# Splitting the output projection's weights half a chunk per attention round

## The chip, the cores and the metric

The kernel runs on one core of a Trainium2 chip. The core has five engines that run side by side and meet through semaphores: TensorE (PE, matrix multiplies and transposes), VectorE (DVE), ScalarE (ACT), GpSimd (POOL) and SyncE (SP, which issues most of the DMAs). The metric is the device time of one execution in microseconds; lower is better.

## The reference

One encoder layer with two kinds of attention side by side, applied to 1024 prompt tokens and 256 sample tokens with the same weights. All arithmetic is float32. What matters here, cut to its core:

```python
n = rms_norm(h, g_mix);  z = n @ w_in               # queries, keys, values of both kinds
oa = diff_attention(qa, ka, va, lam, slopes)        # 4 heads, two softmax maps each, ALiBi distance
oa = rms_norm(oa, g_subln) * (1 - lam_init)
ob = gqa_attention(qb, kb, vb)                      # 8 query heads on 2 key/value heads, rotary positions
h = h + concat([oa, ob]) @ w_out                    # the output projection: this case's stage
h = h + relu(rms_norm(h) @ w_ff1)**2 @ w_ff2        # MLP, 4096 wide
h = h + sigmoid(rms_norm(h) @ w_gate) * (p @ w_proj)
return rms_norm(h, g_final)
```

The output projection multiplies 1280 x 1024 activations by the 1024 x 1024 matrix `w_out`. Its 1024 rows are eight chunks of 128 rows, one for each pair of heads (`ch` 0 to 3 for the differential heads, 4 to 7 for the grouped ones).

## The kernel before, in words

**Precision by splitting.** TensorE multiplies a rounded float32 format (`F32R`) at full rate. To keep float32 accuracy every operand is split into `hi` (the rounded value) and `lo` (what is left), and each product becomes three matmuls: hi x hi, hi x lo, lo x hi. A split of a weight takes a copy on ScalarE and a subtraction on GpSimd.

**Stages.** The input projections come first. Then the attention runs with two kinds of side work woven into it: the rest of the input projection (`qk_rest`) and the output projection (`out_proj`). After the attention the rest of the output projection is woven with the norm and the transposes for the MLP; then the MLP, the gate and the final norm.

**Rounds.** The attention is written out by hand as a list of rounds (L1037 to L1057). A unit is 256 queries of one head; a unit over the 1024 prompt tokens covers four rounds with its transposes (`tr`, L696) and its value matmuls (`av`, L720). Its scores (`sc`, L642) and softmax (L655 or L659, L664 or L667, L675 to L681) run four to seven rounds earlier. The loop runs rounds 3 to 217.

**Filler.** In each round, between the score part and the value part, the loop takes side work from one generator. It may take as much as the round's own matmuls are worth times a ratio: 0.43, and 0.6 from round 160 on (`RATIO`, `RATIO2`, `LATE`). Side work comes in steps of three matmuls of 512 columns, worth 648 ns to the loop (L257). A generator that yields 0.0 ends the side work of that round, and what the round still had to give is forfeited (L1051 to L1053). So each `yield 0.0` means: the rest is for the next round.

**The output projection in two passes.** The first pass (chunks 0, 1, 4, 5) runs when the first half of the heads is done, the second (2, 3, 6, 7) when all are. In a pass, each of ten 128-token tiles takes two halves of 512 output columns; a half is 12 matmuls (four chunks, three products each), then an addition into `h` on VectorE (L942), and a `yield 0.0`. The matmuls are recorded under line 255 (`mm_gen`) with the tile name `pso`. Their PSUM banks come from the pool `pj` (two banks), which the `av` tiles use too.

**A chunk's weights.** `opw_dma` (L862) loads a chunk in two halves of 512 columns; `opw_split` (L874) takes one of five pairs of buffers and splits the two halves: per half a copy on ScalarE (L883) and a subtraction on GpSimd (L884). All of it is written into one round. In the first pass, the constant `Y` puts one `yield 0.0` ahead of the second, third and fourth split, and one ahead of the first tile. Two splits of the second pass are done ahead, inside the first pass, after its tiles 2 and 5 (`ahead`, L948); the last two are done at the start of the second pass, after two `yield 0.0` (L915 to L919). The first two splits of the first pass fall into rounds 104 and 105.

**The order on each engine.** What the code writes first has priority, but the framework orders each engine's instructions itself, with a timeline that it works out when the kernel is built (`schedule_with_timeline_sim`, L1680). So the order seen in the trace can differ from the written one. Loads go through SyncE's queue in order.

**After the rounds.** The loop at L1213 drains what is left of `out_proj`. With each finished tile (`op_done`) a norm (`mlp_norm`, ScalarE and VectorE), and then transposes into the MLP's operands become possible.

Of the kernel before, what the change touches and what calls it, by code (L numbers as in the profile page):

```python
# [40 lines left out]
def f(ap):  # L41
    return ap.bitcast(F32)
# [3 lines left out]
def encoder_kernel(ctx: ExitStack, tc: tile.TileContext, x, xT, pT, w_in, w_out, w_ff1, w_ff2, w_gate, w_proj,  # L46
# [5 lines left out]
    Y = (0, 1, 1)  # L52
# [143 lines left out]
    def slot(tag, shape, dt, name):  # L196
        return slot_pool[tag].tile(shape, dt, tag=tag, name=name, bufs=1)
# [54 lines left out]
    def mm_gen(ps, pairs, step=6):  # L252
        n = len(pairs)
        for i, (a, b) in enumerate(pairs):
            PE.matmul(ps, a, b, start=i == 0, stop=i == n - 1)  # L255
            if i % step == step - 1:
                yield step * ps.free_size() * 0.422  # L257
        if n % step:
            yield (n % step) * ps.free_size() * 0.422
# [280 lines left out]
    def flush():  # L540
        todo, deferred[:] = deferred[:], []
        for fn in todo:
            fn()
# [270 lines left out]
    def qk_rest():  # L814
        w = qk_split(qk_dma(0))
        for n, (h, col, dst, sc) in enumerate(qk_items):
            more = n + 1 < len(qk_items)
            raws = qk_dma(n + 1) if more else None
            wh, wl = w
            for ci, (c0, cn) in enumerate(TCH):  # L820
                ps = pj("psa")
                pr = []
                for k in range(KD):
                    pr += [(wh[k], xh[:, k, c0:c0 + cn]), (wl[k], xh[:, k, c0:c0 + cn]), (wh[k], xl[:, k, c0:c0 + cn])]
                yield from mm_gen(ps[:, :cn], pr, 3)

                def evac(ps=ps, c0=c0, cn=cn, dst=dst, sc=sc, eng=V if LV and not more and ci == 2 else G):
                    hl = zp.tile([P, 2, 512], F32R, tag="zl", name="zl")
                    z = f(hl[:, 1, :cn])
                    V.scalar_tensor_tensor(z, ps[:, :cn], sc, R[:, c0:c0 + cn], op0=ALU.mult, op1=ALU.mult)  # L830
                    S.activation(hl[:, 0, :cn], z, AF.Copy)
                    eng.tensor_tensor(hl[:, 1, :cn], z, f(hl[:, 0, :cn]), op=ALU.subtract)
                    dma(dst[:, :, c0:c0 + cn].rearrange("v p t -> p v t"), f(hl[:, :, :cn]))

                deferred.append(evac)
                yield 0.0
                if ci == 0 and more:
                    w = qk_split(raws)
                elif ci == 0:
                    op_state["w0"] = opw_dma(0, "Q1")  # L840
            qk_done.append(n)
# [3 lines left out]
    def open_out_proj():  # L845
        xs.close()
        fr = pool("fr", side="right")
        open_slots(fr, [f"H{i}" for i in range(7)] + [f"W{i}" for i in range(9)])
        op_state["h"] = [slot(f"H{j}", [P, 2560], F32, "h_sb") for j in range(NT // 2)]
# [3 lines left out]
    def h_row(t):  # L853
        j, half = divmod(TORD.index(t), 2)
        return op_state["h"][j][:, half * D:half * D + D]
# [6 lines left out]
    def opw_dma(ch, tag=None):  # L862
        if tag:
            t = slot(tag, [P, D], F32, "wor")
            raws = [t[:, i * 512:i * 512 + 512] for i in range(2)]
        else:

            n = next(raw_n) % 2
            raws = [op_state["h"][2 * n + i + RO][:, 2 * D:] for i in range(2)]
        for i in range(2):  # L870
            dma(raws[i], w_out[ch * P:(ch + 1) * P, i * 512:i * 512 + 512])
        return raws

    def opw_split(raws):  # L874
        n = next(ow_n) % 5
        if n < 2:
            w = slot(f"H{5 + n}", [P, 2, D], F32R, "ow")
            a, b = w[:, 0], w[:, 1]
        else:
            a, b = (slot(f"W{2 * n - 4 + i}", [P, D], F32R, "ow")[:] for i in range(2))  # L880
        for i, raw in enumerate(raws):
            c = slice(i * 512, i * 512 + 512)
            S.activation(a[:, c], raw, AF.Copy)  # L883
            G.tensor_tensor(b[:, c], raw, f(a[:, c]), op=ALU.subtract)  # L884
        return a, b

    def out_proj(chs, ws, ahead, banks, first):

        mts = {}

        def load_mt(it):
            t = TORD[it]
            mt = mts[it] = slot(("W6", "W7", "W8")[it % 3 if first or it < 6 else it % 2], [P, 4, 2, P], F32R, "mt")
            d = dma(f(mt[:]), md[0 if first else 1][:, :, :, t * P:(t + 1) * P])
            if first:
                with tc.issue_after(d.ins):
                    for t_ in TORD[it + XA if it else 0:it + 1 + XA]:
                        dma(h_row(t_), x[t_ * P:(t_ + 1) * P])

        if first:  # L900
            raws = [op_state.pop("w0"), opw_dma(chs[1]), opw_dma(chs[2])]
            for n in range(4):
                for _ in range(Y[n > 0]):
                    yield 0.0
                ws.append(opw_split(raws.pop(0)))
                if n == 0:
                    raws.append(opw_dma(chs[3], "Q1"))
                    load_mt(0)
        else:
            raws = []  # L910
            for n, ch in enumerate(chs):
                if n >= len(ws):
                    raws.append(opw_dma(ch))
                    if len(raws) == 2:
                        yield 0.0  # L915
                        yield 0.0
                        ws.append(opw_split(raws.pop(0)))
            while raws:
                ws.append(opw_split(raws.pop(0)))  # L919
        nb = 0  # L920
        for it, t in enumerate(TORD):
            while any((ch, t // 2 * 256) not in md_done for ch in chs):
                yield 0.0
            if it not in mts:
                load_mt(it)
            mt = mts.pop(it)
            if it == 0:
                for _ in range(Y[2]):
                    yield 0.0
            for n0 in range(0, D, 512):  # L930
                ps = banks[nb % len(banks)]("pso")
                nb += 1
                pr = []
                for i in range(4):
                    mh, ml = (mt[:, i, v, :] for v in range(2))
                    a, b = (w[:, n0:n0 + 512] for w in ws[i])
                    pr += [(mh, a), (mh, b), (ml, a)]
                yield from mm_gen(ps, pr, 3)

                def evac(ps=ps, t=t, n0=n0):  # L940
                    h = h_row(t)[:, n0:n0 + 512]
                    V.tensor_tensor(h, ps, h, op=ALU.add)  # L942

                deferred.append(evac)
                yield 0.0
            if not first:
                op_done.append(t)
            if ahead and it in (2, 5):  # L948
                ahead.pop(0)()

    w_next = []
    op_done = []

    def side_work():
        yield from qk_rest()
        flush()
        open_out_proj()
        chs2 = (2, 3, 6, 7)
        ahead = []
        for ch in chs2[:2]:  # L960
            box = []
            ahead.append(lambda ch=ch: w_next.append(opw_split(opw_dma(ch))))
        yield from out_proj((0, 1, 4, 5), [], ahead, [pj], True)
        yield from out_proj(chs2, w_next, None, banks2, False)

# [60 lines left out]

    banks2 = [pj]
    side = side_work()
    dma(dst_t, dist)
    owed = PRE  # L1030
# [178 lines left out]
    def first(i):  # L1209
        n_split(i, slice(0, min(HC, DIRECT.get(i, HP) * P)), V)  # L1210

    ahead = [(n, lambda i=i: first(i)) for i, n in FIRST]
# [333 lines left out]
    for ti, t in enumerate(FORD):  # L1546
# [82 lines left out]
        for n0 in range(0, 512 if last else D, 512):  # L1629
            n = slice(n0, n0 + 512)  # L1630
# [54 lines left out]
```

## Time and profile before

| | before |
|---|---|
| median of 3 runs | 1707.38 us (1705.64 to 1707.55) |
| the profiled execution's own time | 1706.36 us |
| its span, first to last instruction | 1704.5 us |
| PE, DVE, ACT, POOL busy | 98%, 69%, 51%, 39% of the span |
| mean granted TensorE clock | 0.997 |

The profile lists instructions by line and engine with their tile names (`out<-in`), their count and their duration in ns, and what ended an engine's idle time (`<-`). A view by windows gives the busy time of each engine between two times, counted from the span's start, with the number of instructions in brackets; the last three columns are the granted TensorE clock (1.00 is full speed), the share of the DMA engines in use, and GB/s. Matmuls are pipelined and their ends are modelled, so a busy PE is not PE at its peak. PEld is the load of weights, which overlaps PE.

### The profile page before, as it was taken

Reading aid. Unit: us, or ns where it says so; the run is one execution under the profiler, and the core shown is the slowest. Engines: PE = TensorE matmul, PEld = TensorE weight load, DVE = VectorE, ACT = ScalarE, POOL = GpSimd, SP = SyncE. Lnnn points to the kernel's source line nnn. Section 1 sums busy time; section 2 is a strip of 40 time slices with the busy share of each in tenths; the row PEclk is TensorE's granted clock in tenths of the full one; section 3 lists DMA queues with packets and bytes.
Section 4 is the critical chain, followed back from the end, with each engine's and each line's share of the span. In section 5 each row is a group of like instructions: output and inputs, shape, how many; then the busy total and the mean of one; then the engine's idle time right before and its main releaser. Section 6 shows DMA issues by size and latency. Waiting matters only on the chain.

```text
span 1704.5 us, 27269 instructions
## 1 busy us (share of the span) xinstructions
PE 1666.3 (98%) x9849; PEld 1487.7 (87%) x9849; DVE 1183.1 (69%) x2115; ACT 868.5 (51%) x1749; POOL 664.6 (39%) x651
## 2 busy tenths in 40 slices
PE   8999999999999999999999999999999999999997
PEld 8998888888788888889999999998888888888886
DVE  7788588787887878568666666665655865445666
ACT  8543377777766767674333233333443333354644
POOL 1124455555753445424655665520533400001441
PEclk9999999999999999999999999999999999999999
DMA  9766843433953624495343334359666465532111
GB/s 323 224 220 240 238 143 119 136 96 105 270 161 118 165 69 125 135 310 181 131 157 127 136 133 146 123 198 373 209 212 199 130 206 189 170 116 72 36 44 50
DMA packets 191867, 278.27 MB, mean 163 GB/s; under 512 B 13675, under 2 KB 121077, under 8 KB 191733
## 3 DMA queue, kind: packets, MB, share of 16 engines
q1 hardware_dynamic: 189988, 271.28, 49.3%
q0 software_dynamic: 1600, 5.24, 1.0%
q8 instruction: 78, 1.28, 0.3%
q14 instruction: 57, 0.46, 0.1%
q10 hardware_dynamic: 144, 0.00, 0.0%
HBM read 182.63 MB, written 88.61 MB: 159 GB/s over the span
## 4 chain that ended last, share of the span: by engine, by line
PE 78%; DVE 8%; ACT 4%; issue 4%; POOL 3%; DMA 3%; SPq 0%; POOLq 0%; ACTq 0%; DVEq 0%
PE psa L255 6%; PE sc L642 5%; PE av L720 5%; PE psb L255 4%; PE pso L255 4%; PE tr L696 4%; PE psv L255 3%; PE psg L1576 2%; DVE pl L707 1%; PE f__16295 L156 1%; PE f__15255 L156 1%; PE f__16637 L156 1%; PE f__15600 L156 1%; PE f__15937 L156 1%; PE f__14906 L156 1%
## 5 line engine op out<-in xcount | busy, mean ns | idle before, releaser
L1373 ACT ACTIVATE ao<-ar 128x1280 fp32r<-128x1280 f32 x56 | 71.4, 1276 | 191.5 <-PE f__16299 L156 37.8
L642 PE MATMUL sc<-kt,qt 128*128 128x512 f32 (+1 forms) x576 | 157.1, 393 | 8.3 <-ACT p L667 5.2
L707 DVE TENSOR_TENSOR pl<-tr,ph 128x512 fp32r<-128x512 f32 x204 | 137.9, 684 | 31.3 <-ACT ph L702 29.4
L1375 DVE TENSOR_TENSOR ao<-ar,ao 128x1280 fp32r<-128x1280 f32 x56 | 93.2, 1665 | 94.2 <-ACT ao L1373 94.2
L702 ACT ACTIVATE ph<-tr 128x512 fp32r<-128x512 f32 x204 | 119.8, 595 | 58.5 <-PE tr L696 51.8
L642 PEld LDWEIGHTS sc<-kt,qt 128*128 128x128 f32 x576 | 99.4, 190 | 26.5 <-ACT p L667 6.7
L696 PE MATMUL tr<-ident,p 128*128 128x128 f32 x768 | 116.1, 274 | 6.2 <-DVE pl L707 5.5
L255 PE MATMUL pso<-ow,mt 128*128 128x512 f32 x480 | 119.3, 395 | 2.0 <-DVE osq L747 1.3
L1576 PE MATMUL psg<-gw,n 128*128 128x512 f32 (+1 forms) x504 | 115.4, 384 | 0.0
L696 PEld LDWEIGHTS tr<-ident,p 128*128 128x128 f32 x768 | 91.7, 141 | 23.2 <-DVE pl L707 9.5
L1576 PEld LDWEIGHTS psg<-gw,n 128*128 128x128 f32 x504 | 90.8, 188 | 19.5
L1094 POOL TENSOR_SCALAR w1r<-w1r,gmlp 128x256 f32<-128x256 f32 x112 | 80.5, 736 | 64.0 <-DMA w1r<-in_w_ff 42.9
L255 PEld LDWEIGHTS pso<-ow,mt 128*128 128x128 f32 x480 | 87.7, 189 | 19.7 <-DVE osq L747 2.0
L720 PE MATMUL av<-ph,vt 128*128 128x256 f32 x544 | 102.4, 289 | 1.0 <-ACT ph L702 0.5
L681 POOL TENSOR_SCALAR p<-p,rl 128x1024 f32<-128x1024 f32 x64 | 76.0, 1189 | 51.1 <-DVE rl L679 45.5
L1167 ACT ACTIVATE w<-w1s 128x512 fp32r<-128x512 f32 x56 | 35.2, 628 | 116.4 <-POOL w1s L1174 53.8
L659 DVE TENSOR_REDUCE mm<-sc 128x1 f32<-128x1024 f32 (+1 forms) x80 | 84.1, 1055 | 9.6 <-PE sc L642 9.2
L720 PE MATMUL av<-pl,vt 128*128 128x256 f32 x408 | 89.9, 302 | 0.0
L720 PEld LDWEIGHTS av<-ph,vt 128*128 128x128 f32 x544 | 82.4, 190 | 6.3 <-DVE osq L747 0.8
L667 ACT ACTIVATE p<-sc,mm 128x1024 f32<-128x1024 f32 x64 | 71.3, 1114 | 25.3 <-DVE mm L659 18.3
L655 DVE CUSTOM_DVE_ANT_0 p<-sc,dist 128x1024 f32<-128x1024 f32 x64 | 77.6, 1218 | 8.2 <-PE sc L642 3.8
L664 ACT ACTIVATE p<-p,mm 128x1024 f32<-128x1024 f32 x64 | 73.5, 1149 | 18.3 <-DVE mm L655 17.3
(1520 smaller groups left out, 4725.0 us busy)
## 6 DMA issues: line engine op xcount, KB each, us to landing
ar<-ad SPq DMA_DIRECT2D x56, 640.0 KB, 4.1
w2r<-in_w_ff SPq DMA_DIRECT2D x56, 512.0 KB, 4.6
qt<-qd SPq DMA_DIRECT2D x160, 128.0 KB, 3.1
ad<-q SPq DMA_DIRECT2D x64, 320.0 KB, 2.8
ad<-qs SPq DMA_DIRECT2D x48, 320.0 KB, 2.2
w1r<-in_w_ff SPq DMA_DIRECT2D x28, 512.0 KB, 4.3
md<-ml SPq DMA_DIRECT2D x40, 256.0 KB, 2.6
mt<-md SPq DMA_DIRECT2D x20, 512.0 KB, 6.0
```

What stands on the lines that cost most here:

```text
L156: PE.matmul(ps, a, b, start=start and i == 0, stop=stop and i == n - 1)
L255: PE.matmul(ps, a, b, start=i == 0, stop=i == n - 1)
L642: PE.matmul(ps[:, h0:h0 + n], shared["q"][:, cc, v, i * P:(i + 1) * P], kt[:, s0 + h0:s0 + h0 + n], start=v == 0, stop=v == 1)
L655: V.tensor_tensor_reduce(out=p[:, :sn], in0=ps[:, :sn], in1=dst_t[:, off:off + sn], scale=SLOPES[idx], scalar=3.0e38, op0=ALU.add, op1=ALU ...
L659: V.tensor_reduce(out=st["m", i][:, 0:1], in_=ps[:, :sn], axis=AX.X, op=ALU.max, negate=True)
L696: PE.transpose(t[:, jj, i * P:(i + 1) * P], st["ws"][i][:, j * P:(j + 1) * P], ident)
L702: S.activation(ph, st["tr", j2], AF.Copy)
L707: V.tensor_tensor(pl, st["tr", j2], f(st["ph", j2][:]), op=ALU.subtract)
L720: PE.matmul(st["av"][:, :256], x_, y_, start=j2 == 0 and n == 0, stop=j2 == nj - 1 and n == len(pr) - 1)
L1094: G.tensor_scalar(raw[:, k], raw[:, k], gmlp[:, 4 * kh + k:4 * kh + k + 1], 1.0, op0=ALU.mult, op1=ALU.mult)
L1375: V.tensor_tensor(ao[:, 1], a, f(ao[:, 0]), op=ALU.subtract)
L1576: ends[:] = [PE.matmul(ps, a, b, start=m == 0, stop=m == len(pr) - 1)]
```

## The change

`opw_split` becomes a generator: after each half (one copy, one subtraction) it yields 0.0, so the second half of a chunk goes to the next round and what follows the split to the round after. All callers pass the yields on: the four splits of the first pass, the two that are done ahead, and the two of the second pass. The yields that `Y` put ahead of three of the first pass's splits are taken out; the one ahead of the first tile stays. No instruction is added or removed.

```diff
@@ opw_split
             c = slice(i * 512, i * 512 + 512)
             S.activation(a[:, c], raw, AF.Copy)
             G.tensor_tensor(b[:, c], raw, f(a[:, c]), op=ALU.subtract)
+            yield 0.0
         return a, b
@@ out_proj
         if first:
             raws = [op_state.pop("w0"), opw_dma(chs[1]), opw_dma(chs[2])]
             for n in range(4):
-                for _ in range(Y[n > 0]):
-                    yield 0.0
-                ws.append(opw_split(raws.pop(0)))
+                ws.append((yield from opw_split(raws.pop(0))))
                 if n == 0:
                     raws.append(opw_dma(chs[3], "Q1"))
                     load_mt(0)
@@
                     if len(raws) == 2:
                         yield 0.0
                         yield 0.0
-                        ws.append(opw_split(raws.pop(0)))
+                        ws.append((yield from opw_split(raws.pop(0))))
             while raws:
-                ws.append(opw_split(raws.pop(0)))
+                ws.append((yield from opw_split(raws.pop(0))))
@@
             if ahead and it in (2, 5):
-                ahead.pop(0)()
+                yield from ahead.pop(0)()
@@ side_work
         for ch in chs2[:2]:
-            box = []
-            ahead.append(lambda ch=ch: w_next.append(opw_split(opw_dma(ch))))
+            def split_ahead(ch=ch):
+                w_next.append((yield from opw_split(opw_dma(ch))))
+
+            ahead.append(split_ahead)
         yield from out_proj((0, 1, 4, 5), [], ahead, [pj], True)
         yield from out_proj(chs2, w_next, None, banks2, False)
```

## The prediction

> **What bounds the kernel now.** I read the page's engine table first.
>
> ```profile
> span 1704.5 us, 27269 instructions
> PE 1666.3 (98%) x9849; PEld 1487.7 (87%) x9849; DVE 1183.1 (69%) x2115; ACT 868.5 (51%) x1749; POOL 664.6 (39%) x651
> ```
>
> TensorE (PE) is the engine nearest to full, but the change touches only one stage, so the next view is busy time by stretch: 440 to 709 is the attention with the output projection as its filler, 709 to 757 the rest of the projection, 757 to 782 the way into the MLP. First all engines, then the projection's matmuls alone (L255).
>
> ```profile
> 440.00:709.00 269.00, 256.26 (x1559) 220.95 (x1558) 214.18 (x403) 186.20 (x388) 132.52 (x142) 0.99 0.49 142
> 709.00:757.00 48.00, 48.00 (x258) 41.15 (x257) 28.94 (x66) 32.24 (x72) 18.47 (x25) 1.00 0.91 293
> 757.00:782.00 25.00, 21.57 (x140) 20.14 (x139) 23.13 (x36) 16.97 (x29) 1.17 (x2) 1.00 0.50 159
> ...
> 440.00:709.00 269.00, 82.08 (x324) 0.99 0.49 142
> 709.00:757.00 48.00, 37.22 (x156) 1.00 0.91 293
> ```
>
> In the attention PE is busy 256.26 of 269.00 us, so it idles 12.74; VectorE (DVE) is second with 214.18. After 709 PE is busy 48.00 of 48.00: a matmul more there is time more. The MLP's entry (757 to 782) follows the projection's last tile and is led by DVE (23.13 of 25.00).
>
> Then the same view cut into stretches of six rounds. A full unit's round has four transposes (L696), so 24 of them mark six rounds; two of those rows show it, the others have 24 to 27. Below them L255's matmuls in such stretches, and all engines in the two stretches that have none.
>
> ```profile
> 521.20:535.20 14.00, 3.54 (x24) 1.00 0.26 77
> 626.70:641.90 15.20, 3.59 (x24) 1.00 0.39 121
> ...
> 478.70:493.40 14.70, 2.90 (x12) 1.00 0.50 158
> 508.10:521.20 13.10, 2.91 (x12) 1.00 0.56 172
> 521.20:535.20 14.00, 0.00 (x0) 1.00 0.26 77
> 553.30:567.40 14.10, 3.18 (x12) 1.00 0.70 178
> 567.40:578.90 11.50, 2.91 (x12) 1.00 0.46 147
> 578.90:594.80 15.90, 6.03 (x24) 1.00 0.62 166
> 594.80:610.30 15.50, 5.88 (x24) 1.00 0.14 39
> 610.30:626.70 16.40, 6.29 (x24) 1.00 0.23 71
> 626.70:641.90 15.20, 6.15 (x24) 1.00 0.39 121
> 641.90:654.40 12.50, 0.00 (x0) 1.00 0.56 148
> ...
> 521.20:535.20 14.00, 12.86 (x78) 10.43 (x77) 13.63 (x31) 11.74 (x27) 6.40 (x8) 1.00 0.26 77
> 641.90:654.40 12.50, 10.97 (x75) 9.55 (x74) 10.34 (x27) 10.38 (x22) 7.27 (x8) 1.00 0.56 148
> ```
>
> With 24 projection matmuls six rounds take (15.90 + 15.50 + 16.40 + 15.20) / 4 = 15.75 us. With 12 they take (14.70 + 13.10 + 14.10 + 11.50) / 4 = 13.35. With none, (14.00 + 12.50) / 2 = 13.25. So above 12 a matmul costs 2.40 / 12 = 0.20 us, PE's price. Below 12 it is nearly free: in 521 to 535 DVE is busy 13.63 of 14.00. Filler taken out of a well-filled stretch shortens it; taken out of a thin one it only leaves PE idle. This is the view the forecast rests on.
>
> **The change, part by part.**
>
> *The instructions are the same.* Sixteen copies and sixteen subtractions remain, and every DMA.
>
> ```profile
> L883 ACT ACTIVATE ow<-h_sb x12: 616/630/638, 442.6 to 642.7; 128x512 fp32r<-128x512 f32 x12
> L884 POOL TENSOR_TENSOR ow<-h_sb,ow x12: 1272/1282/1311, 448.2 to 644.4; 128x512 fp32r<-128x512 f32 x12
> L884 POOL TENSOR_TENSOR ow<-wor,ow x4: 1274/1758/2264, 444.1 to 461.5; 128x512 fp32r<-128x512 f32 x4
> ```
>
> So 0.63 us of ScalarE (ACT) and 1.28 us of GpSimd (POOL) per half chunk, before and after: 0 by themselves.
>
> *More yields of zero.* Each ends the side work of its round and forfeits the round's remaining debt. The first pass's four splits yielded 3 times and now 8 (+5); the two splits ahead 0, now 4 (+4); the second pass's own two gain 4. That is 13 more ended rounds. Rounds 104 to 217 lie in 440 to 709, 269 / 114 = 2.36 us each. Stepping through the loop with the code's own costs (648 ns per step of three matmuls; ratio 0.43, from round 160 on 0.6), I get 109 steps in them before and 92 after. The trace agrees with the first figure: 324 / 3 = 108. Thirteen rounds at 108 / 114 steps would give 12; the other 5 come from the forfeited debt and from where the ends of tiles fall. In this walk the first pass's first matmuls move from round 108 to 113, its last tile ends about nine rounds (21 us) later, and of the second pass's ten tiles about 1.6 instead of 3.3 are done when the rounds end. I take 17 steps, 51 matmuls, moved behind 709; by the smaller count it would be 36.
>
> *Their cost behind 709*: 37.22 / 156 = 0.239 us each, 51 of them 12.2 us, with no cover, since PE is full there. The MLP's entry shifts with the end of the projection and neither gains nor loses. The norms that go with the tiles use ACT and DVE, which have room there (32.24 and 28.94 of 48.00).
>
> *What the attention gains*: between nothing and 51 x 82.08 / 324 = 12.9 us (PE's busy time for them). In the walk, taken six rounds at a time, two stretches fall below the 12-matmul level: the first six rounds lose all they had (6 matmuls) and rounds 194 to 199 lose about 5 of theirs below it. So some 11 of the 51 are worth nothing and 40 are worth 0.20: 8.0 us. I take that because it is what these rows give, and keep 0 and 12.9 as ends.
>
> *The burst at the entry.* This is what the change spreads out.
>
> ```profile
> 441.57 1.16 ACT L883 ACTIVATE ow<-wor 128x512 fp32r<-128x512 f32 x2
> 442.61 0.64 ACT L883 ACTIVATE ow<-h_sb 128x512 fp32r<-128x512 f32 x1
> 444.10 0.63 ACT L883 ACTIVATE ow<-h_sb 128x512 fp32r<-128x512 f32 x1 [0.36 <-DMA h_sb<-in_w_out]
> 445.16 1.11 ACT L667 ACTIVATE p<-sc,mm 128x1024 f32<-128x1024 f32 x1
> 446.42 2.04 PE L642 MATMUL sc<-kt,qt 128*128 128x512 f32 x4 [2.12 <-ACT p L667]
> ...
> 440.00:444.00 4.00, 3.61 (x27) 3.17 (x26) 3.92 (x8) 3.74 (x8) 3.85 (x5) 1.00 0.93 271
> 444.00:448.00 4.00, 1.88 (x7) 1.38 (x6) 2.95 (x5) 3.85 (x7) 4.00 (x4) 0.81 1.01 332
> 448.00:452.00 4.00, 4.00 (x22) 3.52 (x21) 2.15 (x4) 3.42 (x8) 4.00 (x5) 0.76 1.10 354
> ```
>
> Four copies within 3.2 us put the exponential of L667 back, and PE waits 2.12 us for it. Right after, the granted clock is 0.81 and 0.76: (0.19 + 0.24) x 4 = 1.7 us of clock. Price of the burst: 0 to 2.1 + 1.7 = 3.8 us. With one copy a round about half of the ACT work in front of the exponential goes; I take 2.0. Against it: these rounds will have no filler for five rounds more, so PE has less to be busy with.
>
> The Trainium skill, "TensorE: Matmul & The Clock Gate" (section "HAM oscillation — how this bites in real kernels"), says that the clock drops to half only after PE gaps above about 3.4 us. Here a 2.12 us gap goes with the drop, so the trace shows an earlier one than the page has; by the page the drop would not be the gap's and the sum would lose the 1.7 part of the relief (some 1 us of the 2.0).
>
> *Waits and queues.* No wait is added by hand. The loads of the fourth chunk and of the first tile's operands are issued one round (2.4 us) later on SyncE's queue; the matmuls that need them move by five rounds (11.8), which covers it. Without that cover it would cost those 2.4 us.
>
> *Sum*: 12.2 - 8.0 - 2.0 = +2.2 us on the profiled execution's own 1706.36, so 1708.6. The median shown, 1707.38, lies 1.0 above that execution, so 1709.6 among such runs. That is +0.13%. A measurement of this kernel can tell about 0.2%, 3.4 us, from no change.
>
> **The rivals.**
>
> *A. The attention does not shrink (slower).* In the empty stretches DVE sets the pace (13.63 of 14.00). If half of the 51 matmuls come out of stretches at or below 12 per six rounds, the gain is 25 x 0.20 = 5.0, and there is no relief: +7.2, 1714.6. Decided when the stretches after 440 and around 650 to 680 run at 2.2 us a round with no L255 in them. For it: those two stretches are where the new yields sit. Against: the 24-matmul stretches are paid in PE time.
>
> *B. Clock drops (slower).* Longer stretches without filler bring two more half-speed windows of 1.7 us each and the old one stays: 4.2 + 3.4 = +7.6, 1715.0. Against: 521 to 535 had no filler and a granted clock of 1.00. The page above, by its 3.4 us, speaks against it too.
>
> *C. The burst was the cost (faster).* The whole 3.8 goes, and with it the similar wait after the second burst; the attention is PE's throughout and gives back all 12.9:
>
> ```profile
> 644.46 1.19 PE L642 MATMUL sc<-kt,qt 128*128 128x512 f32 x4 [1.08 <-ACT p L667]
> 465.31 0.63 ACT L883 ACTIVATE ow<-h_sb 128x512 fp32r<-128x512 f32 x1 [1.72 <-DMA h_sb<-in_w_out]
> ```
>
> 12.2 - 12.9 - 3.8 - 1.1 = -5.6 at the full, 1701.8; the middle of this case is -4, 1703.4. For it: PE idles only 12.74 us in the attention, so nearly all of its filler is paid for.
>
> *D. It moves less than it says.* The framework orders each engine's queue by its own timeline. The second row shows it: the split ahead of chunk 2 stands in round 135 (some 73 us after 441) and ran at 465.31. If fillers are pulled forward likewise, nothing moves: 1707.4. Against: 324 matmuls before 709 against 327 walked.
>
> **How the numbers follow.** Forecast 0.40, its own range 1706 to 1713: 0.25 of it within 0.2%, 0.15 above. A 0.20, B 0.05: slower. C 0.27: faster. D 0.08: the same. So faster 0.27, same 0.33, slower 0.40. The range reaches down to C's full case and up to the end with no gain in the attention and the relief of 2.0 (12.2 - 2.0 = +10.2, 1717.6): 1701 to 1718.
>
> **What would show it.** Right: about 270 of L255's matmuls before the last transpose of L696 and about 210 behind; the attention ending 8 to 10 us earlier, the last projection tile 2 to 4 us later; no gap over 1 us before L642 near 445. Wrong: an attention of unchanged length (A), clocks under 0.9 elsewhere (B), the same count before the last transpose (D), or DVE's MLP entry longer than 25 us, which the sum holds at nothing.

## The result, and the profile after

The changed kernel takes 1713.14 us (median of 16 runs, 1708.78 to 1715.3) where the kernel before takes 1708.28 (16 runs): a ratio of 1.0028 with a 95% interval of 1.0021 to 1.0035, 4.9 us slower. The forecast was 1709.6, 0.13% slower. Sign and trade are the forecast's, the size is not: the loss lies above 0.2%, and just outside the 1706 to 1713 that the forecast gave for its own case; it is inside the wider range of 1701 to 1718.

The head of the page of the changed kernel. It is the same work: 9849 matmuls, and PE's busy time within 1.3 us of before.

```profile
span 1710.1 us, 27265 instructions
PE 1667.6 (98%) x9849; PEld 1487.5 (87%) x9849; DVE 1178.1 (69%) x2115; ACT 868.2 (51%) x1749; POOL 664.4 (39%) x651
```

The changed kernel by stretches, all engines. The cuts are the attention's last transpose and the projection's last tile in this run.

```profile
440.00:702.00 262.00, 246.50 (x1516) 212.68 (x1514) 208.93 (x390) 181.14 (x376) 133.01 (x142) 0.99 0.47 138
702.00:759.00 57.00, 56.74 (x285) 47.31 (x285) 29.68 (x78) 35.05 (x82) 18.47 (x25) 1.00 0.84 267
759.00:787.00 28.00, 23.28 (x152) 21.68 (x151) 24.95 (x38) 18.87 (x31) 0.77 (x2) 1.00 0.51 174
```

The same view of the projection's matmuls (L255) alone:

```profile
440.00:702.00 262.00, 71.20 (x276) 0.99 0.47 138
702.00:759.00 57.00, 48.90 (x204) 1.00 0.84 267
```

276 projection matmuls stand ahead of the attention's last transpose and 204 behind it, where before it was 324 and 156. So 48 have moved (16 steps; 17 were walked). The attention ends near 702 instead of 709. The stretch behind it is 57 us instead of 48 and PE is as full there as before (56.74 of 57.00).

To compare all kernels I cut each trace at the same four points: the 385th of the 816 transposes of L696 (near 442), the last of them, the last projection matmul, and the 300th matmul of L156 counted from 600 us, which lies inside the MLP. Behind that point every kernel takes 899.0 to 899.4 us. A "drop" is a stretch in which the granted clock is half; most last 3.41 us and cost 1.7. The one that closes every span is left out. The table is worked out from the traces, one execution of each kernel.

| kernel | projection matmuls ahead | attention | behind it | MLP entry | span | drops start at |
|---|---|---|---|---|---|---|
| before | 324 | 266.9 | 45.6 | 50.6 | 1704.5 | 446.5 |
| changed | 276 | 259.5 | 56.5 | 52.4 | 1710.1 | 536.0 |
| e1_yields_only | 276 | 259.3 | 56.2 | 53.9 | 1711.5 | 447.6, 536.4, 771.9 |
| e2_filler_back | 324 | 280.0 | 45.6 | 49.3 | 1724.4 | 440.4 (6.8 us), 464.2, 638.3, 658.8, 710.0 |
| e3_no_yields | 348 | 270.1 | 40.8 | 49.8 | 1703.6 | 447.1 |
| e4_spread | 276 | 256.7 | 56.9 | 53.7 | 1710.9 | 771.8 |
| e5_filler_back | 324 | 278.1 | 45.0 | 52.2 | 1718.2 | 450.0, 654.8 (6.8 us), 777.6 (6.8 us) |
| e6_first_only | 300 | 264.7 | 51.1 | 51.6 | 1711.5 | 450.4, 539.1, 771.2 |
| e7_later_only | 288 | 261.0 | 52.4 | 54.9 | 1710.2 | 767.4 (6.8 us) |
| e8_more_filler | 360 | 280.9 | 41.8 | 53.6 | 1720.6 | 703.3, 778.4 (6.8 us) |
| e9_less_in_attention | 276 of 432 | 259.8 | 45.6 | 50.0 | 1700.4 | none |
| e10_less_behind | 276 of 432 | 258.6 | 52.4 | 55.5 | 1708.4 | 535.6, 733.6 (6.8 us), 778.0 |
| e11_none_spread | 348 | 270.6 | 40.8 | 51.4 | 1704.9 | 447.9 |
| e12_more_behind | 276 of 528 | 260.8 | 65.8 | 47.7 | 1717.6 | 538.1 |

From before to changed that is -7.4 in the attention, +10.9 behind it, +1.8 in the entry and +0.4 after: +5.7, the span's +5.6 but for rounding.

The profiled pair hides one thing: both ran at a mean clock of 0.997. Every timed execution has its mean granted clock on record, and one minus it, times the span, is the time lost. On average that is 6.5 us over the 16 executions of the changed kernel and 4.6 us over the 73 executions of the kernel before that were timed beside the experiments. So about 1.9 of the 4.9 us, about one drop per execution, go with the clock, and about 3 are left for the work.

**The copies did not spread.** ScalarE's copies of weights at the start of the projection, in the changed kernel, in order of time (`...` stands for five more):

```profile
441.61 1.16 ACT L883 ACTIVATE ow<-wor 128x512 fp32r<-128x512 f32 x2
442.65 0.63 ACT L883 ACTIVATE ow<-h_sb 128x512 fp32r<-128x512 f32 x1
443.66 0.63 ACT L883 ACTIVATE ow<-h_sb 128x512 fp32r<-128x512 f32 x1
...
465.44 0.63 ACT L883 ACTIVATE ow<-h_sb 128x512 fp32r<-128x512 f32 x1 [2.34 <-DMA h_sb<-in_w_out]
```

All its copies from `h_sb`, by line (min, median and longest ns, then first and last start in us):

```profile
L883 ACT ACTIVATE ow<-h_sb x12: 614/632/634, 442.7 to 677.7; 128x512 fp32r<-128x512 f32 x12
```

The first copies start at 441.61, 442.65 and 443.66; before it was 441.57, 442.61 and 444.10. The first ten halves all stand within 0.5 us of where they stood. The code puts them a round apart, but each engine's queue is ordered by the framework's own timeline, and that put them back. Only the last six moved, the last from 642.7 to 677.7. What the yields did was to end rounds and take filler away; the first pass's last matmul starts at 667.6 instead of 640.8, and the last copies go with it.

**The drop of the clock moved.** Four stretches of 3.41 us of the changed kernel, two and two in a row:

```profile
443.88:447.29 3.41, 1.77 (x11) 1.33 (x10) 3.08 (x6) 3.36 (x7) 3.41 (x3) 1.00 1.00 325
447.29:450.70 3.41, 3.41 (x28) 3.24 (x27) 2.60 (x4) 3.41 (x8) 3.41 (x4) 1.00 1.10 353
532.63:536.04 3.41, 1.57 (x9) 1.16 (x9) 3.35 (x6) 2.81 (x5) 0.74 (x1) 1.00 0.02 5
536.04:539.45 3.41, 3.41 (x10) 2.65 (x9) 3.41 (x7) 2.13 (x6) 3.15 (x4) 0.50 0.23 77
```

The wait that lies in the third of them, from the view in order of time:

```profile
534.96 1.19 PE L642 MATMUL sc<-kt,qt 128*128 128x512 f32 x4 [1.84 <-ACT p L667]
```

The clock stays at 1.00 behind the burst near 445, where it had dropped before. But a gap of 1.84 us near 534 now brings a drop at 536.04. It does not come from filler that was taken out there: this stretch had none before either (the prediction's row 521.20 to 535.20) and ran at a clock of 1.00, with a wait of 0.35 us for the same exponential. A gap of 1.84 us stands there in all five kernels that have the first pass's yields with nothing else changed in the attention (changed, e1, e6, e10, e12), each time with a drop behind it. It is missing in e7, whose first pass is as before, and in e4. Why the exponential is late there was not traced. In the profiled pair it is one drop before and one after; over all executions the changed kernel loses more.

### The profile page after: what moved, and what is told of

Same layout as the page of the kernel before. It is cut to its first block, busy times and chain, and to the rows that moved or that the text cites. A ratio compares the mean times of both kernels' runs of the same rounds, so it can differ in the third digit from the quotient of the medians.

```text
span 1710.1 us, 27265 instructions
## 1 busy us (share of the span) xinstructions
PE 1667.6 (98%) x9849; PEld 1487.5 (87%) x9849; DVE 1178.1 (69%) x2115; ACT 868.2 (51%) x1749; POOL 664.4 (39%) x651
## 4 chain that ended last, share of the span: by engine, by line
PE 77%; DVE 8%; ACT 5%; issue 5%; POOL 3%; DMA 2%; SPq 0%; POOLq 0%; ACTq 0%; DVEq 0%
PE psa L255 6%; PE sc L642 5%; PE av L720 4%; PE pso L255 4%; PE psb L255 4%; PE tr L696 3%; PE psv L255 3%; PE psg L1577 2%; DVE pl L707 1%; DMA h_sb<-in_w_out 1%; DVE nlo L1202 1%; ACT ph L702 1%; PE f__15255 L156 1%; PE f__16295 L156 1%; PE f__16637 L156 1%
## 5 line engine op out<-in xcount | busy, mean ns | idle before, releaser
L702 ACT ACTIVATE ph<-tr 128x512 fp32r<-128x512 f32 x204 | 120.1, 595 | 64.3 <-PE tr L696 59.1
L255 PE MATMUL pso<-ow,mt 128*128 128x512 f32 x480 | 120.1, 399 | 3.7 <-DVE o L768 1.6
L696 PE MATMUL tr<-ident,p 128*128 128x128 f32 x768 | 116.0, 274 | 6.0 <-DVE pl L707 5.1
L696 PEld LDWEIGHTS tr<-ident,p 128*128 128x128 f32 x768 | 91.0, 140 | 22.6 <-DVE pl L707 8.3
L255 PEld LDWEIGHTS pso<-ow,mt 128*128 128x128 f32 x480 | 88.7, 190 | 22.1 <-DVE o L768 1.9
L655 DVE CUSTOM_DVE_ANT_0 p<-sc,dist 128x1024 f32<-128x1024 f32 x64 | 77.4, 1218 | 11.5 <-PE sc L642 7.3
```

The source lines that it names most:

```text
L655: V.tensor_tensor_reduce(out=p[:, :sn], in0=ps[:, :sn], in1=dst_t[:, off:off + sn], scale=SLOPES[idx], scalar=3.0e38, op0=ALU.add, op1=ALU ...
L696: PE.transpose(t[:, jj, i * P:(i + 1) * P], st["ws"][i][:, j * P:(j + 1) * P], ident)
L702: S.activation(ph, st["tr", j2], AF.Copy)
```

## The experiments

**e1_yields_only: end the rounds, keep the chunk whole.** Both halves go into one round again, and the two yields stand behind them.

```diff
 # the changed kernel, opw_split
             G.tensor_tensor(b[:, c], raw, f(a[:, c]), op=ALU.subtract)
-            yield 0.0
+        yield 0.0
+        yield 0.0
         return a, b
```

> Both halves of a chunk are split in one round, as before the change, and the two yields follow them: the same number of ended rounds as in the changed kernel, without the splitting. Theory 1 (the ended rounds displace the projection's matmuls behind the attention, and that is the whole effect): as the changed kernel, 276 projection matmuls ahead of the last transpose of the attention, 4 to 6 us slower than before. Theory 2 (the halves a round apart cost by themselves): within 2 us of before. Theory 3 (the splitting helps and hides part of the loss): 6 to 8 us slower than before, since the help is gone.

1713.86 us, ratio 1.0029 (1.0018 to 1.0040), as much as the changed kernel, with the same 276 matmuls ahead and stage lengths within 0.3 us in the attention and behind it. The copies start within 0.7 us of the changed kernel's. So the loss comes from the ended rounds; writing the halves apart does nothing that can be measured.

**e3_no_yields: the other way.** The kernel before, without the yields around its splits.

```diff
 # the kernel before
-    Y = (0, 1, 1)
+    Y = (0, 0, 0)
...
                     if len(raws) == 2:
-                        yield 0.0
-                        yield 0.0
                         ws.append(opw_split(raws.pop(0)))
```

> The kernel before without its six yields around the splits and the first tile (Y all zero, the two of the second pass taken out): 348 projection matmuls ahead of the last transpose instead of 324. Theory 1 with the price per matmul of this change (10.9 us behind the attention less 7.4 us in it over 48 matmuls, and 2 us of entry): linear, 24 more bring 2 us of gain; with a price that rises where the rounds are full, 0 to 1 us. Theory 2 and 3: a burst at the entry that is tighter, 1 to 3 us slower than before.

1705.52 us, ratio 0.9989 (0.9979 to 1.0000), and this row of the projection's matmuls ahead of 714:

```profile
L255 PE MATMUL pso<-ow,mt x348: 387/392/685, 450.0 to 712.5; 128*128 128x512 f32 x174
```

24 more matmuls go into the attention. It grows by 3.2 and what is behind shrinks by 4.8, the entry by 0.8. It is the changed kernel's trade run backwards, though the gain is small: the interval reaches up to no change.

**e6_first_only and e7_later_only: the change by halves.** A flag leaves the yields to the first pass's four splits, or to the four later ones (the two ahead and the second pass's two).

```diff
 # the changed kernel; e6: False in the later calls; e7: False in the first pass, with its Y yields back
-    def opw_split(raws):
+    def opw_split(raws, apart=True):
...
-            yield 0.0
+            if apart:
+                yield 0.0
```

> Only the first pass's four splits are halved, the two ahead and the two of the second pass as before the change: 300 matmuls ahead of the last transpose, 24 of the change's 48. Theory 1: half of the change's loss, 2 to 3 us slower than before. Theory 2 (the empty rounds near 650 to 680 us, at the end of the first pass, are the loss): within 1 us of before.

> Only the two splits ahead and the two of the second pass are halved, the first pass as before the change: 288 matmuls ahead of the last transpose, 36 fewer than before. Theory 1: three quarters of the change's loss, 3 to 4 us slower than before. Theory 2: the whole of it, 4 to 6 us.

1712.04 us, ratio 1.0022 (1.0013 to 1.0030), and 1712.69, 1.0031 (1.0019 to 1.0044). Each half alone loses about as much as both, so the losses do not add. The counts (300 and 288 ahead) and the stage lengths in the table fall in line between 324 and 276; the rest goes with the drops: e6 has two more than before, and e7's lasts 6.8 us. All executions say the same: 6.0 and 6.9 us are lost to the clock on average, 4.5 in the kernel before beside them. With that taken off, 2.3 and 3.0 us are left for 24 and 36 matmuls, and 2.9 for the changed kernel's 48.

**e2_filler_back and e5_filler_back: give the filler back by the ratio.** e2 raises the ratio in all rounds up to 159. e5 raises it only from round 104 on, and lets the new yield end the round without forfeiting its debt.

```diff
 # e2, the changed kernel
-    RATIO = 0.43
+    RATIO = 0.46
 # e5, the changed kernel
-            yield 0.0
+            yield 1e-6
...
-(0.0 if r <= 6 else RATIO if r < LATE else RATIO2)
+(0.0 if r <= 6 else RATIO if r < 104 else 0.48 if r < LATE else 0.66)
...
+            if d == 1e-6:
+                break
             if not d:
```

> The changed kernel with the filler's ratio at 0.46 instead of 0.43 up to round 159: the halves stay a round apart and the yields stay, but 324 projection matmuls stand ahead of the last transpose again, as before the change. Theory 1: back to before within 2 us, the attention back at about 709 us. Theory 2: still 4 to 5 us slower than before. Theory 3: 1 to 3 us faster than before.

> The changed kernel, its halves a round apart, with the debt carried over the split's yields and, from round 104 on alone, ratios of 0.48 and 0.66: 324 projection matmuls ahead of the last transpose, as before the change, and nothing moved ahead of round 104 (which the run with the ratio of 0.46 did). Theory 1 (the displaced matmuls are the loss): back to before, within 2 us. Theory 2 (where the yields stand, empty stretches and their clock drops, is the loss, whatever the count): 3 to 5 us slower than before.

1726.03 us, ratio 1.0102 (1.0089 to 1.0115), and 1719.53, 1.0060 (1.0048 to 1.0072). Both have before's 324 matmuls ahead and its 45 us behind, and an attention 11 to 13 us longer. e2 also moves the filler of the rounds ahead of 104, so it isn't a clean test. e5 is, and its trace shows where the time went. ScalarE in order of time, two weight copies and what follows the second:

```profile
648.90 0.63 ACT L883 ACTIVATE ow<-h_sb 128x512 fp32r<-128x512 f32 x1 [2.10 <-DMA h_sb<-in_w_out]
654.57 0.63 ACT L883 ACTIVATE ow<-h_sb 128x512 fp32r<-128x512 f32 x1 [4.15 <-DMA h_sb<-in_w_out]
655.11 0.58 ACT L702 ACTIVATE ph<-tr 128x512 fp32r<-128x512 f32 x1
```

PE at the same place:

```profile
655.74 1.22 PE L720 MATMUL av<-ph,vt 128*128 128x256 f32 x4 [4.05 <-ACT ph L702]
```

All engines in the stretch of that wait and in the one behind it:

```profile
651.35:654.76 3.41, 0.34 (x3) 0.14 (x2) 1.58 (x4) 0.19 (x1) 0.00 (x0) 1.00 0.75 132
654.76:661.59 6.83, 5.85 (x23) 5.36 (x24) 3.94 (x9) 4.42 (x11) 2.45 (x3) 0.50 0.11 38
```

A weight copy stands in ScalarE's queue ahead of the attention's own L702, and the load that it waits for is 4.15 us late. L702 waits behind it, PE waits 4.05 us for L702, and then the clock is half for 6.83 us (3.4 us of work). That is 7.5 us of the 11. "The same count gives back the same time" is refuted: with the count also the places of loads and copies move, and a copy ahead of a late load stalls the attention.

**e8_more_filler: further along.** e3 with a ratio of 0.7 instead of 0.6 from round 160 on.

```diff
 # e3_no_yields
-(0.0 if r <= 6 else RATIO if r < LATE else RATIO2)
+(0.0 if r <= 6 else RATIO if r < 104 else 0.43 if r < LATE else 0.7)
```

> The kernel without the yields around the splits and with a ratio of 0.7 from round 160 on: 360 matmuls ahead of the last transpose, 36 more than before. Theory 1 with one price for all (0.1 us per matmul net): 3 to 4 us faster than before. With a price that rises in full rounds: as the run with 348, 1 to 2 us faster, or worse than it.

1724.37 us, ratio 1.0096 (1.0082 to 1.0111). 360 matmuls ahead lengthen the attention by 14 us instead of some 6. It ends at 726 here, and the waits from 640 to 740 show PE held by the load of the projection's operands (us in total, times, longest):

```profile
PE pso L255 <- DMA mt<-md: 3.6, 3, 2.2
```

These waits and the drop at 703 make part of the excess there. One more wait for such a load, 3.3 us, ends at 756, behind the attention, and a drop of 6.8 us lies in the entry. The rest was not traced. Past e3's 348 nothing was won.

**e4_spread and e11_none_spread: spread the copies in truth.** Each copy is ordered behind the last exponential written ahead of it; e4 in the changed kernel, e11 in e3.

```diff
+                last_exp[:] = [S.activation(... AF.Exp ...)]
...
-            S.activation(a[:, c], raw, AF.Copy)
+            with tc.issue_after(last_exp[0].ins):
+                S.activation(a[:, c], raw, AF.Copy)
```

> The changed kernel with each copy of a split queued on ScalarE behind the exponential that was written last, so that the halves really run a round apart, which the changed kernel's trace doesn't show (its copies at 441.6 to 467.9 us stand where they stood). 276 matmuls ahead of the last transpose, as in the changed kernel. If the burst at the entry costs what the prediction took (2.0 of 3.8 us): the wait of 1.8 us for the exponential near 446 us goes and the kernel is 1 to 3 us faster than the changed one (2 to 4 us slower than before). If the burst costs nothing: as the changed kernel, 4 to 6 us slower than before.

> No yields around the splits (as the run with 348 matmuls, 2 us faster than before) and each copy of a split queued behind the exponential that was written last (as the spread run, 2 to 3 us faster than the changed kernel): if the two gains add, 4 to 5 us faster than before. If the spread's gain was the one clock drop that the changed kernel has at 536 us and this one has not: 2 us faster than before.

e4: 1710.19 us, ratio 1.0012 (1.0003 to 1.0021), 2.9 us better than the changed kernel. e11: 1706.72, 0.9988 (0.9978 to 0.9997), no better than e3. The burst itself stayed in e4 (four copies within 3.1 us of 443.77), so it doesn't test the price of the burst; what did move are the two halves of the first split ahead, from 465 and 468 to 524 and 529. The 2.9 us are not explained by the trace: it is of the slowest of e4's 11 executions (1712.76), with a span of 1710.9. In it the attention is 2.8 us shorter than the changed kernel's (256.7 instead of 259.5), 1.7 of that for want of a drop, but it begins 2.2 us later and the entry has a drop. Whether a real spread would pay is open.

**e9_less_in_attention: the price in the attention.** The kernel before without lo x hi in six tiles of the first pass.

```diff
 # the kernel before
-                yield from mm_gen(ps, pr, 3)
+                if first and 2 <= it < 8:
+                    for i in range(4):
+                        for u_, v_ in pr[3 * i:3 * i + 2]:
+                            PE.matmul(ps, u_, v_, ...)
+                        yield 3 * 512 * 0.422
```

> The kernel before, with 48 matmuls left out of the first pass (the product lo x hi of the activations in tiles 2 to 7; the loop is paid for them as before, so rounds and yields stand where they stood): it measures what the attention gives back for 48 matmuls, with nothing put behind it. If it is the price that the prediction took (0.20 us above 12 per six rounds, nothing below; 8.0 us for 51) and that the change showed (7.4 us for 48): the attention shorter by 6 to 9 us and the kernel faster than before by as much. If every matmul is paid in full: 12 us. If VectorE sets the pace (rival A): 2 to 4 us.

1702.51 us, ratio 0.9957 (0.9944 to 0.9971). 48 matmuls fewer and nothing put behind: the attention is 7.1 us shorter, the rest as before. It also has no drop, worth up to 1.7, so a matmul there costs between 5.4 / 48 = 0.11 and 7.1 / 48 = 0.15 us.

**e10_less_behind and e12_more_behind: the price behind it.** The changed kernel with 48 matmuls fewer (no lo x hi) or 48 more (a fourth product, lo x lo) in the second pass's last six tiles.

```diff
 # the changed kernel
+                if not first and it >= 4:
+                    for i in range(4):
+                        ...   # e10: two products a chunk; e12: four
+                        yield 3 * 512 * 0.422
+                else:
+                    yield from mm_gen(ps, pr, 3)
```

> The changed kernel, with 48 matmuls left out of the second pass behind the attention (the product lo x hi of the activations in its tiles 4 to 9): the number that the change has moved there. If TensorE sets the pace there (0.23 to 0.24 us each): 11 to 13 us faster than the changed kernel, 6 to 8 us faster than before. If the norms, the transposes and GpSimd's transfers set it: 0 to 5 us faster than the changed kernel, not faster than before.

> The changed kernel with work added behind the attention: in the second pass's last six tiles each chunk gets a fourth product, lo by lo, which the kernel leaves out; 48 matmuls of 128x512 more, all behind the last transpose of the attention. Theory 1 (TensorE sets the end behind the attention, so each matmul there costs its 0.23 to 0.24 us): the last projection tile 11 us later than the changed kernel's 758.3, near 769.5, the MLP entry as long as before, and a ratio to the kernel before of 1.0028 + 0.0066 = 1.0094, some 1724 us. Theory 2 (behind the attention the norms and their transfers set the end, as the 3.4 us brought by leaving 48 matmuls out suggest): the projection ends later by as much, but the entry into the MLP gets shorter by half of it or more, and the ratio is 1.0028 to 1.006. If the loss was only the drop of the clock and the wait for the operand load in the run without those matmuls, theory 1 holds here and not there.

e10: 1710.62 us, ratio 1.0008 (0.9998 to 1.0018). e12: 1718.42, 1.0055 (1.0042 to 1.0069). Against the changed kernel's 1.0028 that is 3.4 us won and 4.6 us lost, for matmuls that keep PE busy for 11.5 us (48 x 0.24). All engines from 702 to 800, first the kernel before:

```profile
702.00:800.00 98.00, 94.58 (x572) 85.72 (x571) 67.96 (x135) 59.92 (x124) 33.32 (x47) 1.00 0.77 251
```

The changed kernel:

```profile
702.00:800.00 98.00, 93.03 (x527) 81.99 (x527) 63.09 (x131) 59.16 (x125) 29.05 (x40) 1.00 0.73 238
```

e10, with 48 fewer:

```profile
702.00:800.00 98.00, 88.08 (x490) 77.79 (x489) 67.27 (x136) 59.72 (x125) 35.21 (x44) 0.95 0.76 251
```

e12, with 48 more:

```profile
702.00:800.00 98.00, 97.59 (x540) 86.19 (x539) 61.34 (x125) 59.40 (x122) 24.34 (x34) 1.00 0.68 219
```

PE idles 4.97 us in the changed kernel, 9.92 in e10 and 0.41 in e12. More matmuls fill the idle time at the MLP's entry (52.4 us becomes 47.7); fewer widen it (55.5), and e10 runs at a clock of 0.95 (0.05 x 98 = 4.9 us lost). The 4.6 us rest on five executions, so by the two intervals they may be 2 to 3 us more or less. In e10 PE catches up with a load, as its waits say (line, us in total, times, longest):

```profile
PE pso L940 <- DMA mt<-md: 3.0, 1, 3.0
```

and the clock falls for 6.83 us, in its view by windows:

```profile
730.19:733.60 3.41, 1.21 (x6) 0.67 (x4) 0.88 (x3) 0.19 (x2) 0.00 (x0) 1.00 1.06 358
733.60:740.43 6.83, 6.01 (x18) 5.07 (x19) 2.14 (x10) 3.88 (x11) 0.00 (x0) 0.50 0.94 331
```

The wait of 3.0 us and the 4.9 us of clock together are 7.9, about the 8.1 by which e10's 3.4 fall short of 11.5, so e10 alone doesn't show that something other than PE sets the end. e12 does: it has no drop behind the attention, and its entry is still 4.7 us shorter. So the end behind the attention is not TensorE's alone. The chain of waits says what else holds it, near the projection's last matmuls. The kernel before:

```profile
752.71 4.86 DMA nlo<-nb
...
757.65 0.63 ACT nhi L1200
```

The changed kernel:

```profile
758.00 6.05 DMA nlo<-nb
...
764.12 0.63 ACT nhi L1201
```

e12, where the chain runs through the projection's matmuls instead:

```profile
763.27 7.95 PE pso L941 x35
```

A transfer started by GpSimd, behind the norm of a finished tile, gates the MLP's operand. It starts ahead of the last projection matmul (754.83 before, 758.32 after), so it belongs to an earlier tile than the last. It lands at 757.6 before and 764.0 after. What stands behind such a transfer in the engines' queues is late too, the last tile's own addition into `h` among them. ScalarE's copy for the MLP's operand and then VectorE in the changed kernel:

```profile
759.77 1.49 ACT L1201 ACTIVATE nhi<-nlo 128x1536 fp32r<-128x1536 f32 x1 [1.65 <-DMA nlo<-nt]
...
761.29 1.76 DVE L1202 TENSOR_TENSOR nlo<-nlo,nhi 128x1536 fp32r<-128x1536 f32 x1 [1.69 <-ACT nhi L1201]
763.03 0.68 DVE L941 TENSOR_TENSOR h_sb<-pso,h_sb 128x512 f32<-128x512 f32 x1
```

The same addition in the kernel before:

```profile
756.31 0.68 DVE L942 TENSOR_TENSOR h_sb<-pso,h_sb 128x512 f32<-128x512 f32 x1
```

It starts 1.1 us after the end of the last projection matmul (755.2) before, and 4.3 us after it (758.7) in the changed kernel. When whole tiles move behind the attention, their norms and transfers move with them, and this chain ends 6.5 us later; when matmuls alone are added, as in e12, they fill the time in which PE waits for it. That is how the three runs fit together; the chain was not tested by itself.

## Why the prediction was right, and where its steps were not

- **The trade, right.** Filler moves out of the attention and costs more behind it than it frees. e1 shows that the ended rounds alone do it; e3, which takes more of them out, points the other way (0.9989, up to 1.0000). The walk's count was 51 matmuls, the trace's 48.
- **"Their cost behind 709", 12.2: measured 10.9**, 0.227 a matmul. The size held, the reason was too simple: "PE is full there" is true until the last tile, but e10 and e12 show that 48 matmuls by themselves are worth 3.4 to 4.6 us to the end. That the full price is paid because whole tiles move is the reading that fits these runs; it was not tested by itself.
- **"The MLP's entry ... neither gains nor loses", 0: measured +1.8.** This step failed. The norms were costed by the room that ACT and DVE have, and the transfers behind them weren't costed at all. The size is less sure than the sign: with 1.7 us taken off for each drop, the three kernels with 276 ahead and all the matmuls (changed, e1, e4) have entries of 52.0 to 52.4, before, e3 and e11 of 49.8 to 51.4. Its own test, a longer entry, was the right one to set.
- **"What the attention gains", 8.0: measured 7.4 together with the burst's share.** e9 puts it at 0.11 to 0.15 a matmul with all stretches mixed, where the forecast had 8.0 / 51 = 0.16. That is slightly too high. The rows gave 0.20 above 12 and called it PE's price; PE's busy time in the same rows is 82.08 / 324 = 0.25. That a matmul below 12 is nearly free rests on two stretches, in only one of which an engine is near full (VectorE, 13.63 of 14.00; in the other PE leads with 10.97 of 12.50), and was not tested.
- **"The burst at the entry", 2.0 of relief: nothing is left of it.** This step failed outright. It assumed that halves written a round apart run a round apart. The rival that "it moves less than it says" had the row that spoke against that (the split of round 135 that ran at 465), and was asked only of the matmuls, not of the copies. PE's longest wait near 445 went from 2.12 to 1.64 us, not below the 1 us that it had set as a sign, and the clock there from 0.81 to 1.00. But e1, with the same copies and a wait of 1.67, has its drop there, and the changed kernel has one at 536 instead. Over all executions the clock costs 1.9 us more than before, where the forecast had it cost less.
- **"Waits and queues", 0.** The matmuls that were to move by 11.8 us start 3.7 later (453.22 instead of 449.53); no PE wait above 1 us stands there, so the 0 held, but not by the cover that was named.
- **The sum.** Forecast +2.2, span +5.6. The 3.4 between them: +2.6 in the attention (burst and price), +1.8 at the entry, +0.4 after it, -1.3 behind the attention. So the sign rests on the trade, which was understood; that the time still lies in the stated range owes something to luck, for the range's upper end, 1717.6, was built for an attention that gains nothing and a relief that comes, and neither happened.
- **The rivals.** A took 5.0 out of the attention and no relief: the 7.4 speak against its slow stretches, while its missing relief came true. B had the price of a drop right (1.7) and about half of its size: over all executions about one drop more, not two, and in the profile not where filler was lost, but in the stretch that it had named as harmless. C, whose gain was the burst undone, is out: the burst was not undone, so its price stays untested. D was right of the copies, and wrong of the matmuls.

Over the eight kernels that leave the matmuls and the filler's ratio as they were (348, 324, 300, 288 and 276 ahead), the attention goes from 270.4 (mean of two) to 258.5 (mean of three) and the rest with the entry from 91.4 to 109.9: over 72 matmuls 0.165 us freed and 0.257 us paid each, 0.09 lost. For 48 that is 4.4 us; the medians say 4.9. Both have the drops in them.

## What to carry to other kernels

A change in the code's order relieves an engine only if the order on that engine follows: compare the start times of the very instructions that were meant to move before pricing the relief. Moving filler to behind a stage moves all that hangs on it, here norms and transfers that gate the next stage, so price the chain and not only the matmuls. One profiled execution of each kernel can hide a difference in clock, so compare the granted clock over all of them. And filler can't be added back by a ratio alone: a copy queued ahead of its load (4.15 us late in e5) stops the engine for everything behind it.

## What the runs showed of the hardware

In these traces the clock changes on a fixed grid of windows. The kernel with three drops, e1, in stretches that end and begin where its drops do (PE's busy time is the second number, the clock the third from the end):

```profile
444.21:447.62 3.41, 1.74 (x9) 1.24 (x9) 3.02 (x6) 3.36 (x8) 3.41 (x3) 1.00 1.03 321
447.62:451.03 3.41, 3.41 (x17) 3.29 (x15) 2.19 (x4) 2.83 (x7) 3.41 (x4) 0.50 1.08 361
532.95:536.36 3.41, 1.57 (x9) 1.15 (x8) 3.35 (x6) 2.80 (x6) 0.84 (x1) 1.00 0.02 5
536.36:539.77 3.41, 3.41 (x10) 2.67 (x9) 3.41 (x8) 2.05 (x6) 3.15 (x4) 0.50 0.22 77
768.47:771.88 3.41, 0.96 (x6) 0.65 (x5) 3.37 (x8) 3.41 (x5) 0.00 (x0) 1.00 0.26 77
771.88:775.29 3.41, 3.41 (x16) 3.31 (x14) 3.41 (x4) 2.99 (x7) 0.00 (x0) 0.50 0.01 2
```

The second and the third drop start 88.74 and 324.26 us behind the first, 26.00 and 95.00 times 3.413 us. In every profile with more than one drop (e1, e2, e5, e6, e8, e10) all starts lie on such a grid to within 0.01 us. Between 20 and 1690 us these profiles and the others of this case have 26 drops, and in each PE was busy at most 1.87 us of the 3.41 us window ahead; no window at full clock with less than 1.59 was without a drop behind it. Between these two it went either way: 1.74 brought one in e1, 1.77 none in the changed kernel (the first of its four stretches above). So the length of a gap does not settle it, but how much of it falls into one window: in e8 a gap of 3.29 us that ends at 756.02 lies across two windows, which keep 1.59 and 1.94 us of PE's work, and no drop follows, where 1.84 us brought one in the changed kernel. The grid stands at another place from one profiled execution to the next. That the windows run freely is inferred from this; the grid and the limit, to between 1.59 and 1.87 us of work in a window, are measured. The Trainium skill, "TensorE: Matmul & The Clock Gate" (section "HAM oscillation — how this bites in real kernels"), speaks of gaps above about 3.4 us; the traces agree with the 3.4 us as the length of a window, and differ on the gap, where idle time of about half of it in one window was enough.
